# Seven products in place of eight for pairs of projection units in a two-layer decoder step

## The chip, the cores and the metric
The kernel runs on one core of one Trainium2 chip. The metric is the device time of one execution in microseconds. A core has TensorE for matmuls (PE, with its weight loads listed as PEld), VectorE (DVE), ScalarE (ACT), GpSimd (POOL) and SyncE (SP), which here issues the DMAs. Each engine takes its instructions in order; engines wait for each other by semaphores.

## The reference
Two layers work on 512 prompt tokens and 8 samples together, 520 tokens of 1024 features, in float32. In each layer:
```python
proj = rmsnorm(x, g_mix) @ w_in                  # 1024 -> 5376: u, v, q, k, v of 12 heads, two gates
A = gelu(u) * (tril(W_s) @ rmsnorm(gelu(v)) + b)  # chunks of 128 tokens
B = dilated windowed attention, 3 pairs of (window, dilation), 4 heads each, q and k normed and rotated
x = x + (sigmoid(g_a) * (A @ P_a) + sigmoid(g_b) * (B @ P_b)) @ W_o
c = causal_conv3(rmsnorm(x, g_ffn) @ W_up)        # 1024 -> 5632
x = x + (silu(c_gate) * c_val) @ W_down           # 2816 -> 1024
```
Outputs are x, the new cache rows, the last up-projected rows and the normed v of the samples.

## The kernel before
Features lie on partitions and tokens along the columns, so that a product is made of units of 128 output features by 520 tokens. A float32 product is three products of a faster format: each operand is split into a high part (cast) and a low part (what the cast left out), and a unit multiplies high by high, high by low and low by high. PE's instructions have 260 columns, so a unit over 1024 inputs takes 8 x 3 x 2 = 48 matmuls. The two halves of the tokens lie in two PSUM banks of one tile `acc`.

Weights come in the order of the list `units`: `load_raw` (L181) issues one DMA of 128 output features (512 KB for 1024 inputs) and `split` (L187) makes the high part on ACT (L193) and the low part on DVE (L194), both 1024 columns wide. `feed` (L197) keeps loads three and splits two units ahead. `dense` (L263) runs the matmuls of a unit through `products` (L243, L252). The unit is then taken out of PSUM by DVE: times 1/rms per token for input and up projections (L870, L876, L894, L1051, L1097), as a factor for the projections of the branches (L1062, L1074), added to x for the output and down projections (L1084, L1131). RMSNorm's gain is folded into x before the split (`Norm.feature`, L287), while 1/rms is applied behind the product.

The order of a layer: q, k and v of pair 2 (six units), the v half of the MLP (four), pair 1 (six), the u half (four), pair 0 (six); gates a and the A projection by turns; gates b and the B projection; eight units of W_o; then 22 tiles of the FFN, each a gate unit and a value unit of the up projection, and the down projection in three groups of eight units over 8, 7 and 7 tiles of input, the first two behind the first tile of the next group, the last at the end. Attention of the prompt and of the samples, the spatial gate and the conv history are generators in lanes; `pump` (L215), called before each k of a unit, puts their stages between the matmuls when a clock that counts PE's time says that they are due. A scheduler then orders each engine's list by a simulated timeline; evacuations and splits have priority.

On each FFN tile `up_conv` (L1093) copies ten columns on POOL (L1098), scales on ACT (L1100), adds two taps on DVE (L1102) and eight columns on POOL (L1105); `h_tile` (L1109) applies SiLU (L1120), multiplies (L1121) and splits (L1123 on ACT, L1124 on POOL).

Of the kernel before, what the change touches and what calls it, by code (L numbers as in the profile page):

```python
# [84 lines left out]
def step_kernel(ctx: ExitStack, tc: tile.TileContext, a, o):  # L85
# [59 lines left out]
    units = []  # L145
    groups = ((0, 8), (8, 15), (15, 22))
    for l in range(DEPTH):
        w_in = a["w_in"][l]
# [9 lines left out]
        for j in range(8):
            cols_of(w_in, 0, 8, O_GA + j * 128, 1)
            cols_of(a["w_a_proj"][l], 0, 4, j * 128, 1)  # L160
        cols_of(w_in, 0, 8, O_GB, NGB)
        for j in range(8):
            cols_of(a["w_b_proj"][l], 0, 2, j * 128, 1)
            if NGB + j < 8:
                cols_of(w_in, 0, 8, O_GB + (NGB + j) * 128, 1)
        cols_of(a["w_o"][l], 0, 8, 0, 8)
        for gi in range(3):
            for i in range(*groups[gi]):
                cols_of(a["w_up"][l], 0, 8, i * 128, 1)
                cols_of(a["w_up"][l], 0, 8, DFF + i * 128, 1)  # L170
# [1035 lines left out]
```

## Time and profile before
| | |
|---|---|
| time, median of 3 runs (lowest, highest) | 1585.25 us (1584.99, 1585.29) |
| profiled execution, its span | 1582.3 us, 2.95 under that median, which includes what lies around the span |
| PE busy, matmuls and transposes | 1550.8 us (98%), 12985 instructions |
| DVE, ACT, POOL busy | 934.2, 648.2, 515.6 us (59, 41, 33%) |
| PE's granted clock | 0.9 or more of full speed in all 40 slices |
| DMA | 164.24 MB, 104 GB/s in the mean |

The busy time of an engine includes the time that an instruction already started stands still. Of two neighbours on DVE or PE the end of one overlaps the start of the next, so that durations add up to more than the stretch. Two runs of this kernel agree within 0.02%.

### The profile page before, as it was taken

How to read it: one execution, taken by the hardware profiler on the slowest of the kernel's cores; microseconds unless marked ns; L12 is line 12 of the kernel's file. 1: busy time of each engine (PE TensorE's matmuls, PEld its weight loads, DVE VectorE, ACT ScalarE, POOL GpSimd, SP SyncE). 2: the span in 40 equal slices, each digit the busy share in tenths (PEclk: the TensorE clock that was granted, in tenths of full speed). 3: DMA queues.
4: the chain of work that ended last, by engine and by line, in shares of the span. 5: the costliest groups of instructions: out<-in, count | busy, mean ns of one | idle time of the engine just before them, and what ended most of it. 6: DMA issues, size and time to landing. Idle time of an engine off the chain costs nothing. (4 is left out here: it accounts for less than half of the span.)

```text
span 1582.3 us, 31439 instructions
## 1 busy us (share of the span) xinstructions
PE 1550.8 (98%) x12985; PEld 1522.5 (96%) x12985; DVE 934.2 (59%) x1344; ACT 648.2 (41%) x1155; POOL 515.6 (33%) x677
## 2 busy tenths in 40 slices
PE   8999999899999999999999999998999999999998
PEld 7989899899999999999999999998999999999998
DVE  6576856855466456556437585757655663564652
ACT  5454536334444234334435544552334441442342
POOL 3645453623222012213228272636222220220130
PEclk9999999999999999999999999999999999999999
DMA  7443333424233333332344332433332333323322
GB/s 211 132 115 112 95 107 102 152 78 131 84 94 94 94 94 86 88 95 85 108 113 126 111 125 79 120 113 113 99 115 82 93 94 94 94 84 104 92 73 70
DMA packets 294845, 164.24 MB, mean 104 GB/s; under 512 B 14143, under 2 KB 288335, under 8 KB 294687
## 3 DMA queue, kind: packets, MB, share of 16 engines
q1 hardware_dynamic: 294703, 162.24, 35.0%
q8 instruction: 102, 1.67, 0.4%
q14 instruction: 40, 0.33, 0.1%
HBM read 154.66 MB, written 10.36 MB: 104 GB/s over the span
## 5 line engine op out<-in xcount | busy, mean ns | idle before, releaser
L252 PE MATMUL acc<-t,whi 128*128 128x260 f32 x7776 | 1276.4, 285 | 11.1 <-DVE t L1051 8.7
L252 PEld LDWEIGHTS acc<-t,whi 128*128 128x128 f32 x7776 | 1070.7, 189 | 18.4 <-issue 11.6
L252 PE MATMUL acc<-t,wlo 128*128 128x260 f32 x3888 | 785.5, 284 | 0.0
L252 PEld LDWEIGHTS acc<-t,wlo 128*128 128x128 f32 x3888 | 600.4, 189 | 1.4 <-issue 0.7
L193 ACT CAST whi<-raw 128x1024 fp32r<-128x1024 f32 (+3 forms) x268 | 260.5, 973 | 457.4 <-PE acc L252 287.5
L194 DVE TENSOR_TENSOR wlo<-raw,whi 128x1024 fp32r<-128x1024 f32 (+3 forms) x268 | 323.0, 1206 | 40.3 <-ACT whi L193 22.9
L1097 DVE TENSOR_TENSOR t<-acc,t 128x520 f32<-128x520 f32 x88 | 61.5, 699 | 158.2 <-PE acc L252 158.2
L1098 POOL COPY ut<-t 128x10 f32<-128x10 f32 x88 | 30.9, 351 | 364.5 <-DVE t L1097 361.1
L1102 DVE SCALAR_TENSOR_TENSOR t<-t,cwc,t 128x511 f32<-128x511 f32 (+1 forms) x176 | 131.6, 749 | 4.9 <-ACT t L1100 1.8
L1131 DVE TENSOR_TENSOR x<-acc,x 128x520 f32<-128x520 f32 x48 | 33.5, 700 | 148.2 <-PE acc L252 148.2
L1124 POOL TENSOR_TENSOR t<-t,t 128x520 fp32r<-128x520 f32 x44 | 58.9, 1339 | 127.1 <-ACT t L1123 127.1
L300 POOL TENSOR_TENSOR t<-t,t 128x520 f32<-128x520 f32 x25 | 44.0, 1762 | 110.1 <-ACT t L299 107.5
L1100 ACT ACTIVATE t<-t,vcol,cwc 128x520 f32<-128x520 f32 x88 | 72.5, 824 | 5.8 <-DVE t L1097 5.5
L1123 ACT CAST t<-t 128x520 fp32r<-128x520 f32 x44 | 27.6, 627 | 115.2 <-DVE t L1121 115.2
L506 POOL TENSOR_TENSOR t<-t,t 128x128 f32<-128x128 f32 x96 | 56.7, 619 | 18.8 <-DVE ss L499 18.2
L1105 POOL TENSOR_TENSOR t<-t,hc 128x8 f32<-128x8 f32 x88 | 45.4, 515 | 49.7 <-ACT t L1100 49.7
L1120 ACT ACTIVATE t<-t 128x520 f32<-128x520 f32 x44 | 28.1, 639 | 81.1 <-DVE t L1102 81.1
L1075 POOL TENSOR_TENSOR t<-t,t 128x520 f32<-128x520 f32 x16 | 23.6, 1482 | 80.5 <-DVE t L1074 80.5
L653 ACT ACTIVATE t<-t,stat 128x128 f32<-128x128 f32 (+1 forms) x96 | 40.1, 420 | 22.9 <-DVE stat L650 22.7
L136 POOL TENSOR_TENSOR rr<-ss,mhalf 128x8 f32<-128x8 f32 (+1 forms) x30 | 49.0, 1632 | 0.0
L1051 DVE TENSOR_TENSOR t<-acc,t 128x520 f32<-128x520 f32 x32 | 22.2, 695 | 43.7 <-PE acc L252 43.7
L775 POOL TENSOR_TENSOR t<-t,t 128x512 f32<-128x512 f32 x24 | 35.1, 1473 | 30.3 <-DMA t<-in_cache_kv_w_dram 25.4
(195 smaller groups left out, 1172.2 us busy)
## 6 DMA issues: line engine op xcount, KB each, us to landing
raw<-in_w_up_dram SPq DMA_DIRECT2D x88, 512.0 KB
raw<-in_w_in_dram SPq DMA_DIRECT2D x84, 512.0 KB
raw<-in_w_down_dram SPq DMA_DIRECT2D x32, 448.0 KB
t<-in_cache_kv_w_dram SPq DMA_DIRECT2D x48, 256.0 KB
raw<-in_w_o_dram SPq DMA_DIRECT2D x16, 512.0 KB
raw<-in_w_down_dram SPq DMA_DIRECT2D x16, 512.0 KB
raw<-in_w_a_proj_dram SPq DMA_DIRECT2D x16, 256.0 KB
out_dram<-t SPq DMA_DIRECT2D x15, 256.0 KB
```

The source lines that it names most:

```text
L136: pool.tensor_tensor(out, in_, mhalf[: in_.shape[0], :n], op=ALU.pow)
L193: act.copy(hi[:, :nk], r)
L194: eng.tensor_tensor(lo[:, :nk], r, hi[:, :nk].bitcast(F32), op=ALU.subtract)
L252: mm = pe.matmul(acc[:, h, :H2], w[:, k], m[:, h * H2 : h * H2 + H2], start=(k == 0 and i == 0), stop=(k == last and i == 2),)
L300: eng.tensor_tensor(self.ssum[i], self.ssum[i], sq, op=ALU.add)
L506: pool.tensor_tensor(s4[:, i, :, s : s + 32], q4[:, i, :, d : d + 32], ts_[:n, i : i + 1, s : s + 32].to_broadcast([n, 4, 32]), op=ALU.mult,)
L653: act.activation(S[:, hp], S[:, hp], AF.Exp, bias=nmx[:, i : i + 1], accum_out=stat[:, 4 + i : 5 + i])
L1097: dve.tensor_tensor(v2(up), acc, rb, op=ALU.mult)
L1100: act.activation(cv, up, AF.Identity, scale=cwc[:, 2, i : i + 1], bias=vcol[:, 32 + i : 33 + i])
L1102: dve.scalar_tensor_tensor(cv[:, s:TP], up[:, : TP - s], cwc[:, j, i : i + 1], cv[:, s:TP], op0=ALU.mult, op1=ALU.add)
L1105: pool.tensor_tensor(cv[:, TP:], cv[:, TP:], hc[:, :, m], op=ALU.add)
L1124: pool.tensor_tensor(lo, cg, hi.bitcast(F32), op=ALU.subtract)
```

## The change
Where two units of 128 output features share their input, they can be computed together. The 1024 inputs are halved (1 and 2: k 0 to 3 and 4 to 7), the 520 tokens are halved (260 each), and the weights of the two units form a 2 x 2 matrix of blocks of 512 x 128. `dense2` computes seven products of such blocks, each of 4 x 3 matmuls of 260 columns into one PSUM bank: 84 matmuls for two units. The weights' side takes four sums of blocks (S1 to S4, on POOL), the input's side takes the sums of halves of x made once for each norm (`Norm.operands`), and the outputs are put together by additions out of PSUM on DVE, the first by a copy on ACT. Because sums of tokens' halves would mix two tokens' 1/rms, x is multiplied by it before the split on this path.

Pairs are: q, k and v of attention pairs 1 and 0, the MLP halves, both gates, and FFN tiles 4 to 21 (value and gate unit together): 36 a layer. The other units stay as they were, in blocks of at most four k: q, k, v of pair 2, the projections of the branches, W_o, FFN tiles 0 to 3, W_down. The down projection is cut into groups over 7, 5, 5 and 5 tiles, and the units of the first three groups are laid between later tiles: two behind each of the tiles 8 to 11, two behind 13 to 16, and 1, 1, 2 and 4 behind 18 to 21. PSUM is now five single banks `acc` and three `tp` (which take the scores too). The rings of weights hold six blocks of 4 x 128 columns, high and low, and nine raw blocks.

```diff
 def acc_tile():
-    return ps.tile([128, 2, 512], F32, tag="acc", name=nm("acc"))
+    return ps.tile([128, 512], F32, tag="acc", bufs=5, name=nm("acc"))[:, :H2]
...
+    for g, grp in enumerate(groups):
+        if grp[0] == "s":
+            _, w, c0, c1 = grp
+            loads.extend(((w, 0, 4, c0), (w, 0, 4, c1), (w, 4, 4, c1), (w, 4, 4, c0)))
+            blocks.extend((g, n) for n in ("11", "S2", "12", "S3", "22", "S1", "S4"))
+            continue
...
-    def split(u, eng=dve):
+    def split(eng=dve):
+        g, name = blocks[st["split"]]
+        def summed(p, q, op):
+            s = wp.tile([128, 4, 128], F32, tag="sum", bufs=4, name=nm("sum"))
+            with urgent():
+                pool.tensor_tensor(s, p, q, op=op)
+            return s
+        if groups[g][0] == "u":
+            r = next_raw()
+        else:
+            if name == "11":
+                d = parts4[g] = {n: next_raw() for n in ("11", "21", "22", "12")}
+                d["S1"] = summed(d["21"], d["22"], ALU.add)
+                d["S2"] = summed(d["S1"], d["11"], ALU.subtract)
+                d["S3"] = summed(d["11"], d["21"], ALU.subtract)
+                d["S4"] = summed(d["12"], d["S2"], ALU.subtract)
+            r = parts4[g][name]
...
         with urgent():
             act.copy(hi[:, :nk], r)
             eng.tensor_tensor(lo[:, :nk], r, hi[:, :nk].bitcast(F32), op=ALU.subtract)
...
+    def feed():
+        while st["split"] < len(blocks) and (st["split"] < RING or st["split"] - RING in st["used"]):
+            split()
+        while st["raw"] < len(loads) and st["raw"] < st["taken"] + RAWS - 4:
+            load_raw()
...
+    def dense2(X, g0, g1, done0, done1):
+        finish("n", "x")
+        def product(name, i, out):
+            hi, lo = block(g, name)
+            acc = acc_tile()
+            for k in range(4):
+                triple((hi[:, k], lo[:, k]), X[i][k], [acc], k == 0, k == 3)
+            used(g, name)
+            with urgent():
+                out(acc)
+        def plus(out, p):
+            return lambda acc: dve.tensor_tensor(out, acc, p, op=ALU.add)
+        a11, a12, a21, a22 = g0[:, :H2], g0[:, H2:], g1[:, :H2], g1[:, H2:]
+        def both(acc):
+            dve.tensor_tensor(a22, acc, a22, op=ALU.add)
+            dve.tensor_tensor(a12, acc, a12, op=ALU.add)
+        product("11", 1, lambda acc: act.copy(a11, acc))
+        product("S2", 6, plus(a12, a11))
+        product("12", 2, plus(a11, a11))
+        product("S3", 7, plus(a22, a12))
+        product("22", 4, plus(a21, a22))
+        product("S1", 5, both)
+        done1(g1)
+        product("S4", 3, plus(a12, a12))
+        done0(g0)
...
+        def operands(self):
+            for s in range(7):
+                    if s < 4:
+                        for xn, m in ((x1, s), (x2, s + 4)):
+                            dve.scalar_tensor_tensor(xn, x[:, m], vcol[...], self.rbc, op0=ALU.mult, op1=ALU.mult)
+                        pool.tensor_tensor(d[:, b1], x1[:, b2], x1[:, b1], op=ALU.subtract)
+                        pool.tensor_tensor(d[:, b2], x2[:, b2], x1[:, b2], op=ALU.subtract)
+                        high((s, 1), x1[:, b1])
+                        high((s, 2), x2)
+                    if 0 <= s - 1 < 4:
+                        low((k, 1), x1[:, b1], 1)
+                        low((k, 2), x2, 2, 3)
+                        dve.tensor_tensor(x1[:, b1], x2[:, b2], d[:, b1], op=ALU.subtract)
+                        dve.tensor_tensor(x1[:, b2], x2[:, b1], x1[:, b1], op=ALU.subtract)
+                        high((k, 5), d)
...
-            acc = dense(xs)
-            with urgent():
-                dve.tensor_tensor(v2(g), acc, rb, op=ALU.mult)
-            act.activation(g, g, AF.Tanh, scale=0.5)
+            dense2(X, *g, half, half)
...
+            elif i < NSTD:
+                for j in range(2):
+                    dense(xs, lambda _, *accs, j=j: unit(j, *accs))
+            else:
+                dense2(X, tmp(), tmp(), lambda up: have(1, up), lambda up: have(0, up))
...
+        for op, i, *m in ffn:
+            if op == "up":
+                h_tile(i)
+            else:
+                into_x(m[0], down(i))
```

How the lists of the engines change, at three places. DVE in the up projection, before: `wlo` is the low part of a unit's weights, `acc` the PSUM tile, `t` a work tile; L1097 takes a unit out, L1102 adds the conv's taps, L1121 multiplies.
```order
L1121 TENSOR_TENSOR t_5414<-t_5414,t_5415 128x520
L1097 TENSOR_TENSOR t_5603<-acc_5554,t_5259 128x520
L194 TENSOR_TENSOR wlo_5613<-raw_5548,whi_5612 128x1024
L1102 SCALAR_TENSOR_TENSOR t_5546<-t_5603,cwc,t_5546 128x511
L1102 SCALAR_TENSOR_TENSOR t_5546<-t_5603,cwc,t_5546 128x510
L1097 TENSOR_TENSOR t_5665<-acc_5616,t_5259 128x520
L194 TENSOR_TENSOR wlo_5683<-raw_5610,whi_5682 128x1024
L1102 SCALAR_TENSOR_TENSOR t_5547<-t_5665,cwc,t_5547 128x511
L1102 SCALAR_TENSOR_TENSOR t_5547<-t_5665,cwc,t_5547 128x510
L1121 TENSOR_TENSOR t_5546<-t_5546,t_5547 128x520
L1097 TENSOR_TENSOR t_5735<-acc_5686,t_5259 128x520
```
After, at tile 6 of layer 0: L272 is the low part of a block, from a raw block or a sum; L403, L408 and L409 are the additions out of PSUM, L1331 the taps, L1348 the product.
```order
L1331 SCALAR_TENSOR_TENSOR t_7128<-t_6977,cwc,t_7128 128x510
L272 TENSOR_TENSOR wlo_7213<-sum_7180,whi_7212 128x512
L1348 TENSOR_TENSOR t_7104<-t_7104,t_7128 128x520
L272 TENSOR_TENSOR wlo_7231<-raw_7031,whi_7230 128x512
L272 TENSOR_TENSOR wlo_7249<-sum_7182,whi_7248 128x512
L403 TENSOR_TENSOR t_7140<-acc_7164,t_7140 128x260
L403 TENSOR_TENSOR t_7140<-acc_7198,t_7140 128x260
L403 TENSOR_TENSOR t_7141<-acc_7216,t_7140 128x260
L403 TENSOR_TENSOR t_7141<-acc_7234,t_7141 128x260
L272 TENSOR_TENSOR wlo_7274<-raw_7029,whi_7273 128x512
L408 TENSOR_TENSOR t_7141<-acc_7252,t_7141 128x260
L409 TENSOR_TENSOR t_7140<-acc_7252,t_7140 128x260
```
Low parts come twice as often and half as wide, and two or three of them stand between the additions of one pair.

POOL in the up projection, before: L1098 and L1105 are the ten and the eight columns, L1124 the low part of a tile.
```order
L1124 TENSOR_TENSOR t_5939<-t_5810,t_5938 128x520
L1098 COPY ut_5260<-t_5999 128x10
L1105 TENSOR_TENSOR t_5942<-t_5942,hc_451 128x8
L1098 COPY ut_5260<-t_6061 128x10
L1105 TENSOR_TENSOR t_5943<-t_5943,hc_451 128x8
L1124 TENSOR_TENSOR t_6071<-t_5942,t_6070 128x520
L1098 COPY ut_5260<-t_6131 128x10
L1105 TENSOR_TENSOR t_6074<-t_6074,hc_451 128x8
```
After, at the same place: L254 are the sums of blocks, L1327, L1334 and L1351 what L1098, L1105 and L1124 were.
```order
L254 TENSOR_TENSOR sum_7017<-sum_7015,raw_6633 128x512
L1327 COPY ut_6098<-t_6815 128x10
L1334 TENSOR_TENSOR t_6941<-t_6941,hc_262 128x8
L254 TENSOR_TENSOR sum_7019<-raw_6633,raw_6864 128x512
L1327 COPY ut_6098<-t_6814 128x10
L1334 TENSOR_TENSOR t_6965<-t_6965,hc_262 128x8
L254 TENSOR_TENSOR sum_7021<-raw_6868,sum_7017 128x512
L254 TENSOR_TENSOR sum_7178<-raw_7027,raw_7029 128x512
L1351 TENSOR_TENSOR t_6974<-t_6941,t_6973 128x520
L254 TENSOR_TENSOR sum_7180<-sum_7178,raw_6870 128x512
L1327 COPY ut_6098<-t_6978 128x10
L1334 TENSOR_TENSOR t_7104<-t_7104,hc_262 128x8
```
Four sums stand among the five instructions that a tile had.

POOL in layer 0's input projections, where the MLP halves and the samples' attention run: before, L506 and L136 belong to the norm of q and k, L897 and L898 to GELU, L775 to the products with cached rows.
```order
L897 TENSOR_SCALAR t_977<-t_977 128x520
L506 TENSOR_TENSOR t_997<-t_996,t_659 128x4x32 x4
L898 TENSOR_TENSOR t_977<-t_977,t_855 128x520
L136 TENSOR_TENSOR rr_1034<-ss_1033,mhalf 128x8
L775 TENSOR_TENSOR t_1076<-t_1076,t_1006 128x512
L897 TENSOR_SCALAR t_1091<-t_1091 128x520
L898 TENSOR_TENSOR t_1091<-t_1091,t_983 128x520
L775 TENSOR_TENSOR t_1148<-t_1148,t_1006 128x512
L775 TENSOR_TENSOR t_1180<-t_1180,t_1006 128x512
L775 TENSOR_TENSOR t_1203<-t_1203,t_1006 128x512
```
After, L1104 and L1105 are GELU's, L957 the products with cached rows, and L254 the sums of the next pairs.
```order
L254 TENSOR_TENSOR sum_1470<-raw_1182,sum_1466 128x512
L1104 TENSOR_SCALAR t_1363<-t_1363 128x520
L957 TENSOR_TENSOR t_1383<-t_1383,t_1281 128x512
L1104 TENSOR_SCALAR t_1389<-t_1389 128x520
L1105 TENSOR_TENSOR t_1363<-t_1363,t_1114 128x520
L254 TENSOR_TENSOR sum_1751<-raw_1476,raw_1478 128x512
L1105 TENSOR_TENSOR t_1389<-t_1389,t_1113 128x520
L957 TENSOR_TENSOR t_1458<-t_1458,t_1281 128x512
L254 TENSOR_TENSOR sum_1753<-sum_1751,raw_1184 128x512
L254 TENSOR_TENSOR sum_1755<-raw_1184,raw_1476 128x512
L957 TENSOR_TENSOR t_1501<-t_1501,t_1281 128x512
L254 TENSOR_TENSOR sum_1757<-raw_1480,sum_1753 128x512
```
The sums stand between products with cached rows and GELU's instructions.

## Rows read from the trace of the kernel before
**Rows 1.** The page: span; busy us and share of each engine; the casts of the weights
```profile
span 1582.3 us, 31439 instructions
...
PE 1550.8 (98%) x12985; PEld 1522.5 (96%) x12985; DVE 934.2 (59%) x1344; ACT 648.2 (41%) x1155; POOL 515.6 (33%) x677
...
L193 ACT CAST whi<-raw 128x1024 fp32r<-128x1024 f32 (+3 forms) x268 | 260.5, 973 | 457.4 <-PE acc L252 287.5
...
```

**Rows 2.** Stretches of layer 0: length, busy us (instructions) by engine, PE clock, DMA
```profile
...
53.00:210.00 157.00, 151.93 (x1301) 144.09 (x1300) 105.39 (x177) 78.25 (x195) 81.14 (x90) 1.00 0.36 107
210.00:309.00 99.00, 94.61 (x803) 90.66 (x803) 74.28 (x145) 46.76 (x119) 62.36 (x105) 0.99 0.40 121
309.00:369.00 60.00, 58.32 (x486) 57.93 (x486) 35.42 (x49) 20.61 (x34) 13.60 (x13) 1.00 0.34 98
...
470.00:801.00 331.00, 330.92 (x2767) 330.66 (x2766) 179.77 (x216) 120.25 (x151) 67.51 (x95) 1.00 0.32 94
...
```

**Rows 3.** The same view of two stretches of 6 us
```profile
...
300.00:306.00 6.00, 1.97 (x17) 1.79 (x16) 5.82 (x8) 1.19 (x3) 6.00 (x7) 1.00 0.67 207
306.00:312.00 6.00, 6.00 (x39) 6.00 (x39) 6.00 (x8) 0.59 (x1) 2.49 (x2) 0.72 0.08 22
...
```

**Rows 4.** Timeline at 327 us: start, duration, engine, line, operands, idle time before it
```profile
...
327.05 1.31 POOL L1075 TENSOR_TENSOR t<-t,t 128x520 f32<-128x520 f32 x1 [18.56 <-DVE t L1074]
...
327.11 2.34 DVE L194 TENSOR_TENSOR wlo<-raw,whi 128x1024 fp32r<-128x1024 f32 x1 [0.20 <-ACT whi L193]
...
```

**Rows 5.** Timeline at 381 us
```profile
...
380.26 1.23 DVE L194 TENSOR_TENSOR wlo<-raw,whi 128x1024 fp32r<-128x1024 f32 x1 [0.19 <-ACT whi L193]
...
381.40 0.75 DVE L292 SCALAR_TENSOR_TENSOR t<-x,vcol,t 128x520 fp32r<-128x520 f32 x1
381.46 1.86 POOL L300 TENSOR_TENSOR t<-t,t 128x520 f32<-128x520 f32 x1 [10.01 <-ACT t L299]
...
```

**Rows 6.** Timeline at 455 us
```profile
...
455.33 1.33 POOL L1124 TENSOR_TENSOR t<-t,t 128x520 fp32r<-128x520 f32 x1 [2.93 <-ACT t L1123]
...
456.01 0.70 DVE L1097 TENSOR_TENSOR t<-acc,t 128x520 f32<-128x520 f32 x1 [1.42 <-PE acc L252]
...
```

**Rows 7.** POOL on work tiles: least, middle and greatest ns of a line
```profile
...
L506 POOL TENSOR_TENSOR t<-t,t x96: 447/476/1517, 67.3 to 1014.3; 128x128 f32<-128x128 f32 x96
...
L1124 POOL TENSOR_TENSOR t<-t,t x44: 1297/1316/1845, 434.5 to 1536.9; 128x520 fp32r<-128x520 f32 x44
...
L775 POOL TENSOR_TENSOR t<-t,t x24: 1260/1290/2297, 88.8 to 1030.0; 128x512 f32<-128x512 f32 x24
...
```

**Rows 8.** Groups by line and shape, whole span: count, busy us, mean ns, idle before
```profile
...
L194 DVE TENSOR_TENSOR wlo<-raw,whi 128x1024 fp32r<-128x1024 f32 x204 | 269.7, 1322 | 38.6 <-ACT whi L193 22.5 <-issue 1.3 <-PE acc L252 0.8
...
L1097 DVE TENSOR_TENSOR t<-acc,t 128x520 f32<-128x520 f32 x88 | 61.5, 699 | 158.2 <-PE acc L252 158.2
...
L644 DVE TENSOR_TENSOR t<-sc,cst 128x256 f32<-128x256 f32 x36 | 13.5, 411 | 0.0
...
L194 DVE TENSOR_TENSOR wlo<-raw,whi 128x512 fp32r<-128x512 f32 x16 | 11.4, 715 | 0.5 <-ACT whi L193 0.5
...
```

**Rows 9.** The same view of 53 to 210 us, DVE and then POOL
```profile
...
L515 DVE TENSOR_TENSOR t<-t,t 128x256 f32<-128x256 f32 x16 | 9.2, 601 | 1.6 <-POOL t L506 1.6
...
L518 DVE TENSOR_TENSOR t<-t,t 128x512 f32<-128x512 f32 x8 | 6.9, 867 | 0.0
L900 DVE SCALAR_TENSOR_TENSOR t<-t,t 128x520 f32<-128x520 f32 x8 | 6.7, 838 | 7.7 <-ACT t L899 7.7
...
L335 DVE TENSOR_TENSOR t<-t,t 128x520 fp32r<-128x520 f32 x4 | 2.8, 694 | 2.0 <-ACT t L334 2.0
...
L506 POOL TENSOR_TENSOR t<-t,t 128x128 f32<-128x128 f32 x32 | 20.0, 655 | 5.2 <-DVE ss L499 4.9
...
L775 POOL TENSOR_TENSOR t<-t,t 128x512 f32<-128x512 f32 x8 | 12.3, 1537 | 13.4 <-DMA t<-in_cache_kv_w_dram 8.6 <-PE tp L977 4.8
...
L556 POOL TENSOR_TENSOR t<-t,t 32x128 f32<-32x128 f32 x2 | 0.9, 450 | 0.2
...
```

More of the change, by code (lines that the diff above doesn't have):

```diff
@@ L142, in step_kernel @@
     cwc = cp.tile([128, 3, 88], F32, name="cwc")
-    units = []
-    groups = ((0, 8), (8, 15), (15, 22))
+    groups = []
+    pieces = ((0, 7), (7, 12), (12, 17), (17, 22))
+    ffn = []
+    for i in range(22):
+        ffn.append(("up", i))
+        for g, i0, ns in ((0, 8, (2, 2, 2, 2)), (1, 13, (2, 2, 2, 2)), (2, 18, (1, 1, 2, 4))):
+            if 0 <= i - i0 < 4:
+                ffn.extend(("down", g, sum(ns[: i - i0]) + j) for j in range(ns[i - i0]))
+    mix = ("g0", "g1", "b0", "g2", "b1", "b2", "g3", "b3", "b4", "b5", "b6", "b7")
@@ L147, in step_kernel, with one, two @@
     for l in range(DEPTH):
         w_in = a["w_in"][l]
-        def cols_of(w, k0, k1, c0, n):
-            units.extend((w, k0, k1 - k0, c0 + i * 128) for i in range(n))
+        def one(w, k0, nk, *cs):
+            groups.append(("u", w, k0, nk, cs))
+        def two(w, c0, c1):
+            groups.append(("s", w, c0, c1))
         for p in (2, 1, 0):
-            for off in (O_Q, O_K, O_VV):
-                cols_of(w_in, 0, 8, off + p * 256, 2)
-            if p:
-                cols_of(w_in, 0, 8, O_V if p == 2 else O_U, 4)
@@ L158, in step_kernel @@
[L158 to L170, printed above, removed]
-                if gi > 0 and i == groups[gi][0]:
-                    cols_of(a["w_down"][l], *groups[gi - 1], 0, 8)
@@ L173, in step_kernel @@
-        cols_of(a["w_down"][l], *groups[2], 0, 8)
-    raws, splits = {}, {}
-    st = {"raw": 0, "split": 0, "u": 0, "now": 0.0, "last": -9.0, "pin": False}
-    RAW_AHEAD, SPLIT_AHEAD = 3, 2
+            c = [off + p * 256 + h * 128 for off in (O_Q, O_K, O_VV) for h in range(2)]
+            if p == 2:
+                n = 3 if l == 0 else 2
+                one(w_in, 0, 8, *c[:n])
+                for i in range(n, 6):
+                    one(w_in, 0, 8, c[i])
+            else:
+                for i in range(0, 6, 2):
+                    two(w_in, c[i], c[i + 1])
@@ new lines, in qkv_units, with unit, normed @@
+            first = [0]
+            def unit(j, *accs):
+                g = tmp()
+                normed(g, accs)
+                have(first[0] + j, g)
+            dense(xs, unit, l == 0)
+            if l == 0:
+                t = tps()
+                pe.transpose(t[:, :104], vrow[:104], ident[:104, :104])
+                act.copy(vcol[:, 16:], t[:, :104])
+            for i in range(n, 6):
+                first[0] = i
+                dense(xs, unit)
+        def normed(dst, accs):
```

474 lines of the change are left out of this document (291 added, 183 removed).

## The prediction
> **What bounds the kernel now.** I read the busy times first: PE 98% of the span, DVE 59%, ACT 41%, POOL 33% [rows 1]. Then the stretches of layer 0 between landmarks: B (two MLP halves and the q, k, v of pairs 1 and 0, with most of the attention beside them) from 53 to 210 us, C (gates a) to 309, D (gates b) to 369, and the up and down projections [rows 2]. There PE is the limit nearly everywhere: 330.92 us for 2767 instructions from 470 to 801, or 119.6 ns each. So what is taken off PE is gained, as long as the other engines follow. The second thing to see is where they don't: from 300 to 306 us DVE is busy for 5.82 and POOL for all of 6 us, PE does 17 instructions, and in the 6 us behind that PE's granted clock is 0.72 [rows 3]. POOL's and DVE's work is thus not free where both are full at once.
>
> Why they can be full at half their own load is in three stretches of the timeline. POOL began a sum of 520 columns at 327.05, DVE a subtraction of 1024 at 327.11, and this took 2.34 us [rows 4] where the same instruction takes 1.23 [rows 5]: it lost 1.11, the rest of POOL's 1.31. At 381.46 it is the other way round: POOL needs 1.86 beside a DVE instruction of 0.75 that began 0.06 before, so it lost some 0.55 [rows 5]. In both cases one had the other wait until about 0.13 us before its own end. DVE instructions that read PSUM and one tile of SBUF don't take part: L1097 takes its 0.70 inside a POOL sum of 1.33 [rows 6]. So there is one resource for POOL's reads and DVE's instructions with two SBUF operands; I call it the shared port. An instruction holds it for its undisturbed time less 0.13: DVE 1.10 for 1024 columns, 0.55 for 512, 0.28 for 256, 0.62 for the three-operand form of 520; POOL 1.16 for 512 and 1.18 for 520 (1.290 and 1.316 in the middle), 0.32 for 128 (0.447 at least) [rows 7].
>
> **The change, part by part.**
>
> *PE.* 36 pairs of units a layer go from 96 matmuls to 84: 72 x 12 = 864 fewer, at 119.6 ns 103.3 us, or 1.435 us a pair (11.48 to 10.05). The transposes and all other matmuls stay. The Trainium skill (TensorE: Matmul & The Clock Gate, "Back-to-back issue gap") has columns/2.4 + 2.5 ns for the gap of single warm matmuls, 110.8 for 260 columns. By that 864 would be worth 95.7 us; the row is slower, and decides.
>
> *DVE, per pair.* Seven low parts of 512 columns in place of two of 1024: 7 x 0.715 - 2 x 1.322 = +2.4 [rows 8]. Eight additions of 260 columns out of PSUM in place of two of 520 at 0.70; 260 are not in the trace, so between half of 0.70 (+1.4) and 0.45 (+2.2); I take 0.41, the row of 256 [rows 8]: +1.9. 72 x 4.3 = 310 us.
>
> *Operands.* For each of four norms 4 steps with two three-operand products, two sums of 260 and four low parts: about 4.8 us of DVE each by the same rows, 77 us in all. DVE comes to 934 + 310 + 77 = 1320 us before overlap of neighbours, 85% of what I predict. The first pairs wait for these operands behind only three and four plain units in the input projections, behind eight in the up projections. Bounds 0 and 10 us a layer, I take 3.5, since in layer 0 DVE has 26 us of work (19 of operands, 7 for three plain units) for 17 us of PE there, but a pair starts with the operand that is ready first.
>
> *POOL.* Four sums of 512 a pair at 1.29: 5.2 us, 72 x 5.2 = 371 us, and 32 subtractions of 260 for the operands at half of 1.316, 21: from 516 to some 908. *ACT.* Half-sized casts and a copy out of PSUM; even if the 260.5 us of casts doubled [rows 1], ACT would be at 59%. It is covered by PE.
>
> *Shared port.* A pair holds it 7 x 0.55 + 4 x 1.16 = 8.5 us of its 10.05; two plain units hold it 2.2 of 11.48. This term decides. Stage by stage:
>
> B holds ten pairs, 85 us. Beside them stand DVE's eight groups of the side work, L515 to L335, 60 instructions, 26 us by the holds above, and POOL's eleven, L506 to L556, 75 instructions, 42 us [rows 9]. (POOL's powers, L136, are left out: they read at most eight columns. If they held it, 17 us more.) Sum 153 us. PE had 151.9 busy us and will have 137.5. So B is bound by the port at 153 if it never idles; full use is not to be had with two queues in order, and I take B at its old 157: its 14.4 us are lost.
>
> C and D hold eight pairs. POOL was busy 62 of 99 us in C, more than in B (81 of 157), and far less in D [rows 2]. I give these pairs half of their 11.5 us; the ends are nothing and all.
>
> Up projections: a tile with a pair holds 8.5 and four more three-operand products (2.5), a product of 520 (0.57), and POOL's low part with its small ones (1.4): 13.0 of 10.05 us of PE. The tiles 4 to 7 have no down units between them: 4 x 2.95 = 12 over, of which what was prepared ahead (six blocks, at most 8.6 us, with DVE full already) pays a little: 10 us lost. Tiles 8 to 21 have 24 down units between them, which cost PE 98 and the port 19: 14 x 13.0 + 19 = 201 of 239 us. These follow PE; that is the cover which hides the sums.
>
> Weights come in halves of 256 KB: the same bytes, at a DMA share of about a third [rows 2], hidden. Down units are cut 7, 5, 5, 5 for 8, 7, 7: as many matmuls, 32 additions in halves (0.82) for 24 (0.70) a layer, beside PE. PSUM: five banks of one product each (1.44 us) against an evacuation of 0.41; a wait of DVE of up to 4 us is covered.
>
> Sum: -103.3 + 28.7 (B, both layers) + 11.5 (C, D) + 20 (tiles 4 to 7) + 7 (operands) = -36.1. The profiled span is 1582.3, 2.95 under the median of 1585.25 that includes what lies around it; the change touches neither start nor end by more than 3 us. Prediction **1549 us**; by itself this case lies between 1520 and 1580.
>
> **The rivals.**
>
> *PE alone.* The waits at the port fall into slack: five banks, six blocks ahead. Then only the operands cost: -103 + 7, 1489 us. For it: 98% PE now, and single port waits of 1.1 us beside which PE went on [rows 4]. Against it: 153 us asked in 137.5.
>
> *The port at 85%.* Slower. DVE takes its instructions in order, so an evacuation stands behind a low part that waits for a POOL sum, which waits for the port; while both wait, the port idles. At 85% B takes 153/0.85 = 180 (+23 on 157), C and D about their old 159 (+2), tiles 4 to 7 take 52/0.85 = 61 for 46 (+15), the rest keeps its -20, operands +3.5: +23 a layer, 1631 us. It turns slower than before below about 90%. For it: [rows 3], where both were full and PE nearly stood. After a halt of 4 us the clock of 0.72 costs some 1.7 us on top. Against it: while POOL holds the port, DVE has 3.3 us of evacuations a pair that don't need it. The Trainium skill (SBUF — State Buffer, "Who interferes with whom") says that of such a DVE instruction and a GpSimd one that reads SBUF the later is blocked fully. [Rows 4, 5] agree: 2.34 for 1.23. Were it only a slowdown like the mean of 1.322 against 1.23, the case before would hold.
>
> *Sums behind a late transfer.* POOL's queue now has the sums of the next pair between the products with cached rows (L775 before). If these wait for their DMA as they do now, PE waits too, up to some 13 us a layer: 1575 us. For it: they were the port's neighbours already. Against: six blocks of lead.
>
> **How the numbers follow.** Forecast 0.43, PE alone 0.19, late transfer 0.09, port at 85% 0.29. The range of 8 in 10 goes from 1490 (half of the PE case is left out below) to 1633 (a third of the slow case above). A change under 0.2% (3.2 us) can't be told from none. Faster: 0.42 + 0.19 + 0.05 = 0.66; within 0.2%: 0.05; slower: 0.29.
>
> **What would show it.** PE with 864 fewer instructions at 119 to 121 ns between them in the down units. In B PE waiting again and again for ACT's or DVE's halves of the weights, DVE over 85% busy, its low parts of 512 at 0.9 or more in the mean in place of 0.68 to 0.72, and POOL's sums at 1.5 or more; B about 157 us long. Tiles 4 to 7 at some 12.5 us, tiles with two down units at PE's time. It is wrong if B shrinks by its 14 us (PE alone), if DVE's low parts keep 0.7 us while POOL is half busy, or if the tiles with down units halt too (port at 85%).

## The result: 11.7% slower

| | before | changed |
|---|---|---|
| time, median (lowest, highest), 4 runs each | 1585.2 us (1584.99, 1585.29) | 1770.61 us (1765.81, 1772.38) |
| ratio, 95% interval | | 1.1166 (1.115 to 1.1182) |

The forecast was 1549 us, between 1490 and 1633. The time lies above the range, on the side of the rival "port at 85%", and beyond its 1631. The page of the changed kernel, against [rows 1]: span, busy time by engine, then DVE's busy tenths and PE's granted clock in 40 slices.

```profile
span 1768.7 us, 33620 instructions
...
PE 1554.2 (88%) x12121; PEld 1504.1 (85%) x12121; DVE 1522.6 (86%) x2472; ACT 865.2 (49%) x1775; POOL 997.2 (56%) x997
...
DVE  6999979899589988999787998897984998889993
...
PEclk9889789989989899999989897888999899999999
```

PE has the 864 instructions fewer that were counted, and is not less busy (1554.2 for 1550.8 us): it worked at a lower granted clock (0.929 of full speed in the mean) and stood still for 214.5 us, where it stood for 31.5 before. DVE, forecast at 1320 us, is busy for 1522.6. The stretches of layer 0 show where, as [rows 2] do for the kernel before: A (q, k, v of pair 2), B, C, D, then F (the first four up tiles, plain), G (tiles 4 to 7) and H (tiles 8 to 21 with down units). The border of a stretch is the last evacuation of its last unit (an evacuation takes a finished product out of its PSUM bank). Columns: length, busy us (instructions) of PE, weight loads, DVE, ACT, POOL, then PE's clock and DMA.

```profile
0.00:76.20 76.20, 55.87 (x360) 52.35 (x361) 57.09 (x89) 37.50 (x67) 35.95 (x32) 0.87 0.52 138
76.20:271.20 195.00, 160.17 (x1177) 146.77 (x1176) 178.76 (x278) 98.88 (x252) 140.73 (x130) 0.86 0.32 92
271.20:388.10 116.90, 96.52 (x753) 90.08 (x752) 103.31 (x199) 55.52 (x144) 87.82 (x121) 0.93 0.34 103
388.10:442.80 54.70, 54.66 (x458) 54.45 (x457) 51.77 (x91) 29.57 (x57) 31.25 (x23) 1.00 0.39 112
485.50:553.20 67.70, 52.81 (x405) 51.95 (x404) 56.77 (x87) 30.67 (x52) 30.92 (x33) 0.90 0.20 58
553.20:610.80 57.60, 46.80 (x337) 45.84 (x336) 54.08 (x75) 28.19 (x49) 35.68 (x36) 0.88 0.24 70
610.80:848.60 237.80, 229.24 (x1874) 228.64 (x1873) 219.31 (x347) 119.57 (x209) 123.52 (x120) 0.98 0.32 92
```

B took 195 us where I had said 157. DVE was busy for 92% of it. PE's busy 160.17 us at a clock of 0.86 would be 137.7 at the full one (an estimate from that row), which is what was forecast (137.5); so some 22 us are lost to the clock, and 34.8 us PE stood still. Only D (54.7 for 60.0) is shorter by what its pairs save.

The groups by shape show DVE's low parts and POOL's sums, to be read beside [rows 7, 8]: count, busy us, mean ns.

```profile
L272 DVE TENSOR_TENSOR wlo<-raw,whi 128x512 fp32r<-128x512 f32 x336 | 332.7, 992 | 69.3 <-ACT whi L271 57.2 <-PE acc L333 6.8 <-DMA raw<-in_w_up_dram 2.3
L272 DVE TENSOR_TENSOR wlo<-sum,whi 128x512 fp32r<-128x512 f32 x288 | 263.5, 920 | 20.5 <-ACT whi L271 19.9
L403 DVE TENSOR_TENSOR t<-acc,t 128x260 f32<-128x260 f32 x360 | 149.2, 420 | 13.8 <-PE acc L333 6.2 <-ACT t L411 4.5
...
L254 POOL TENSOR_TENSOR sum<-raw,raw 128x512 f32<-128x512 f32 x144 | 222.3, 1544 | 172.8 <-DVE wlo L272 124.1 <-DMA raw<-in_w_up_dram 19.5 <-issue 15.2
```

A low part of 512 takes 0.92 to 0.99 us in the mean in place of 0.72, a sum 1.54 in place of 1.29. In the trace of the changed kernel the 206 low parts of 512 that met no POOL instruction took 0.68 us in the mean, and the 128 that began while POOL ran a sum 1.46. The additions out of PSUM, which read only one tile of SBUF, take their 0.42 (estimate 0.41).

How such waits reach PE is seen in B at 205 us. The timeline (start, duration, engine and line; in brackets the idle time before it), with PE's next product as its last line:

```profile
205.38 0.68 DVE L272 TENSOR_TENSOR wlo<-sum,whi 128x512 fp32r<-128x512 f32 x1
...
206.13 1.65 POOL L254 TENSOR_TENSOR sum<-raw,raw 128x512 f32<-128x512 f32 x1 [0.96 <-DVE wlo L272]
206.59 1.75 DVE L272 TENSOR_TENSOR wlo<-sum,whi 128x512 fp32r<-128x512 f32 x1
...
208.25 0.69 DVE L1107 SCALAR_TENSOR_TENSOR t<-t,t 128x520 f32<-128x520 f32 x1
208.47 1.60 POOL L254 TENSOR_TENSOR sum<-raw,sum 128x512 f32<-128x512 f32 x1 [0.68 <-POOL sum L254]
208.98 1.64 DVE L1214 SCALAR_TENSOR_TENSOR t<-t,t 128x520 f32<-128x520 f32 x1
...
211.31 0.70 DVE L538 TENSOR_TENSOR t<-t,t 128x520 fp32r<-128x520 f32 x1 [0.69 <-ACT t L537]
...
211.93 0.89 DVE L403 TENSOR_TENSOR t<-acc,t 128x260 f32<-128x260 f32 x2
...
212.41 0.80 PE L333 MATMUL acc<-t,whi 128*128 128x260 f32 x2 [6.36 <-DVE t L403]
```

Two evacuations of 0.42 stand at 211.93 in DVE's queue, behind a low part and a product that each lost 0.9 to 1.1 us to a POOL sum, and PE halts for 6.36 us until they free a bank. In F the same happens with the operands (layer 0, 513 us):

```profile
512.87 1.56 POOL L254 TENSOR_TENSOR sum<-raw,sum 128x512 f32<-128x512 f32 x1 [0.72 <-DMA raw<-in_w_up_dram]
...
513.23 2.71 DVE L495 TENSOR_TENSOR t<-t,t 128x520 fp32r<-128x520 f32 x3
...
515.86 1.42 DVE L506 SCALAR_TENSOR_TENSOR t<-x,vcol,t 128x520 f32<-128x520 f32 x2
...
519.82 2.25 DVE L495 TENSOR_TENSOR t<-t,t 128x260 fp32r<-128x260 f32 x4
...
521.99 0.75 DVE L1098 TENSOR_TENSOR t<-acc,t 128x260 f32<-128x260 f32 x2
522.46 0.80 PE L333 MATMUL acc<-t,whi 128*128 128x260 f32 x2 [8.95 <-DVE t L1098]
```

Nine microseconds of operands (L495, L506) and other work run on DVE ahead of two evacuations that take 0.75 us together. Around these two halts PE's granted clock was 0.60 (204.5 to 212.5 us) and 0.75 (511.0 to 522.5).

Evacuations by DVE are only one of the ways. What PE waited for, over the whole kernel and then in B of layer 0 (us in total, times, longest):

```profile
PE acc L333 <- ACT t L411: 41.6, 16, 4.1
PE acc L333 <- DVE t L1098: 40.9, 11, 8.9
PE tp L794 <- DVE t L703: 32.8, 14, 3.6
PE acc L333 <- DVE t L403: 21.7, 9, 6.4
```
```profile
PE tp L794 <- DVE t L703: 9.8, 4, 3.1
PE acc L333 <- DVE t L403: 8.9, 2, 6.4
PE tp L812 <- ACT t L873: 5.5, 1, 5.5
```

In B most halts are before attention's transposes and products (`tp`): 12 of the 34.8 us for the normed q and k, which DVE makes (L703, L704), and 13 for a `tp` bank that DVE (L826, L1205) or ACT (L873, L852) has yet to empty. Evacuations of `acc` account for 9. In G all 10.8 us of halts are for ACT's copy L411, the first evacuation of a pair. All four times it stands in ACT's queue behind a cast (L1350) that waits for a product of DVE (L1348), here at 575 us:

```profile
574.09 0.69 DVE L1348 TENSOR_TENSOR t<-t,t 128x520 f32<-128x520 f32 x1
...
574.81 0.63 ACT L1350 CAST t<-t 128x520 fp32r<-128x520 f32 x1 [1.93 <-DVE t L1348]
575.34 0.37 ACT L411 COPY t<-acc 128x260 f32<-128x260 f32 x1
...
575.76 0.80 PE L333 MATMUL acc<-t,whi 128*128 128x260 f32 x2 [4.12 <-ACT t L411]
```

So a late DVE reaches PE in three ways: by what it empties, by what it makes for attention, and through ACT's queue.

### The profile page after: what moved, and what is told of

It is laid out like the page before. It is cut to its first block, busy times and chain, and to the rows that moved or that the text cites. A ratio compares the mean times of both kernels' runs of the same rounds, so it can differ in the third digit from the quotient of the medians.

```text
span 1768.7 us, 33620 instructions
## 1 busy us (share of the span) xinstructions
PE 1554.2 (88%) x12121; PEld 1504.1 (85%) x12121; DVE 1522.6 (86%) x2472; ACT 865.2 (49%) x1775; POOL 997.2 (56%) x997
## 5 line engine op out<-in xcount | busy, mean ns | idle before, releaser
L333 PE MATMUL acc<-t,whi 128*128 128x260 f32 x7216 | 1339.4, 293 | 111.0 <-ACT t L411 41.6
L333 PEld LDWEIGHTS acc<-t,whi 128*128 128x128 f32 x7216 | 1123.3, 197 | 127.6 <-ACT t L411 45.5
L333 PE MATMUL acc<-t,wlo 128*128 128x260 f32 x3608 | 950.9, 290 | 0.0
L333 PEld LDWEIGHTS acc<-t,wlo 128*128 128x128 f32 x3608 | 666.9, 196 | 0.5 <-issue 0.2
L272 DVE TENSOR_TENSOR wlo<-raw,whi 128x512 fp32r<-128x512 f32 (+2 forms) x464 | 418.3, 904 | 89.2 <-ACT whi L271 77.0
L271 ACT CAST whi<-raw 128x512 fp32r<-128x512 f32 (+2 forms) x464 | 265.5, 576 | 320.7 <-PE acc L333 249.3
L254 POOL TENSOR_TENSOR sum<-raw,raw 128x512 f32<-128x512 f32 x144 | 222.3, 1544 | 172.8 <-DVE wlo L272 124.1
L272 DVE TENSOR_TENSOR wlo<-sum,whi 128x512 fp32r<-128x512 f32 x288 | 263.5, 920 | 20.5 <-ACT whi L271 19.9
L271 ACT CAST whi<-sum 128x512 fp32r<-128x512 f32 x288 | 177.4, 620 | 129.2 <-PE acc L333 116.9
L1331 DVE SCALAR_TENSOR_TENSOR t<-t,cwc,t 128x511 f32<-128x511 f32 (+1 forms) x176 | 171.7, 994 | 2.3 <-ACT t L1329 1.8
L403 DVE TENSOR_TENSOR t<-acc,t 128x260 f32<-128x260 f32 x360 | 149.2, 420 | 13.8 <-PE acc L333 6.2
L254 POOL TENSOR_TENSOR sum<-sum,raw 128x512 f32<-128x512 f32 x72 | 105.5, 1465 | 60.5 <-issue 43.2
L254 POOL TENSOR_TENSOR sum<-raw,sum 128x512 f32<-128x512 f32 x72 | 110.2, 1530 | 21.7 <-issue 7.7
L1351 POOL TENSOR_TENSOR t<-t,t 128x520 fp32r<-128x520 f32 x44 | 69.1, 1570 | 68.2 <-ACT t L1350 53.4
L1327 POOL COPY ut<-t 128x10 f32<-128x10 f32 x88 | 41.6, 472 | 106.1 <-DVE t L408 74.4
L835 ACT ACTIVATE t<-t,stat 128x128 f32<-128x128 f32 (+1 forms) x96 | 40.2, 423 | 31.1 <-DVE stat L832 31.1
L1350 ACT CAST t<-t 128x520 fp32r<-128x520 f32 x44 | 27.6, 627 | 55.6 <-DVE t L1348 55.5
L537 ACT CAST t<-t 128x520 fp32r<-128x520 f32 (+1 forms) x40 | 19.8, 496 | 68.3 <-DVE t L1214 26.9
```

Of the source, the lines that this page charges most:

```text
L254: pool.tensor_tensor(s, p, q, op=op)
L271: act.copy(hi[:, :nk], r)
L272: eng.tensor_tensor(lo[:, :nk], r, hi[:, :nk].bitcast(F32), op=ALU.subtract)
L333: mm = pe.matmul(b, wi, xi[:, h * H2 : h * H2 + H2], start=start and i == 0, stop=stop and i == 2,)
L403: return lambda acc: dve.tensor_tensor(out, acc, p, op=ALU.add)
L835: act.activation(S[:, hp], S[:, hp], AF.Exp, bias=nmx[:, i : i + 1], accum_out=stat[:, 4 + i : 5 + i])
```

## Experiments

The theory after the result: POOL's sums (which hold DVE off the port) and the lumps of operands (many DVE instructions in one go) fill DVE's queue; evacuations stand in it; PE halts, and the clock falls. Rivals: the rest of the rewrite costs (half blocks, five banks of one product); the mere amount of DVE's work; the wait for a sum as an operand.

All runs at a glance. Stretches are added over both layers, from the profiled execution of each (W_o, 85 us in all of them, is left out); the border of F and G shifts a little where DVE is late.

| kernel | A | B | C+D | F | G | H and last downs | time, us |
|---|---|---|---|---|---|---|---|
| changed | 128.6 | 386.1 | 345.8 | 135.9 | 114.1 | 567.7 | 1770.6 |
| 1 all plain | 95.5 | 315.3 | 322.1 | 95.8 | 92.0 | 580.4 | 1593.4 |
| 2 pairs in input only | 131.3 | 385.7 | 340.8 | 96.0 | 92.3 | 582.4 | 1721.0 |
| 3 pairs in up only | 98.4 | 315.3 | 322.6 | 136.4 | 112.8 | 568.5 | 1646.8 |
| 4 no sums | 123.3 | 337.6 | 323.0 | 129.6 | 88.9 | 543.2 | 1637.9 |
| 5 operands not urgent | 131.6 | 381.8 | 341.4 | 135.9 | 110.4 | 569.2 | 1762.6 |
| 6 no operands | 101.8 | 388.0 | 342.4 | 96.0 | 112.4 | 569.4 | 1702.3 |
| 7 sums on DVE | 127.0 | 366.2 | 332.4 | 135.2 | 110.8 | 556.0 | 1720.6 |
| 8 neither sums nor operands | 97.4 | 333.7 | 312.0 | 96.0 | 88.8 | 543.5 | 1563.9 |
| 9 sums nobody uses | 136.3 | 379.4 | 347.8 | 137.5 | 118.0 | 575.9 | 1787.4 |
| 10 as 8, three of seven blocks split | 98.9 | 309.0 | 301.4 | 95.8 | 80.8 | 541.5 | 1519.4 |
| 11 pairs in tiles 8 to 21, operands in a lump | 97.5 | 315.1 | 322.8 | 128.1 | 92.3 | 553.3 | 1602.1 |
| 12 the same, operands spread, 8 | 98.0 | 313.4 | 323.3 | 112.9 | 84.7 | 558.4 | 1583.4 |
| 13 the same, spread, 11 | 97.3 | 314.2 | 322.5 | 108.8 | 79.6 | 560.6 | 1574.7 |
| 14 as 13, sums on POOL | 97.0 | 314.9 | 324.4 | 108.8 | 85.8 | 568.4 | 1585.9 |

Runs 1 to 12 are one run each beside one of the kernel before (1584.2 to 1585.3), 13 and 14 medians of 5 and 11 runs; the stretches of 14 are from its slowest run (1591.8). The four runs of the changed kernel spread over 6.6 us, so a few microseconds between single runs show nothing. Runs 4, 6, 8, 9 and 10 leave sums or operands out, or don't use them: their times are prices of parts, not of a usable kernel.

**1, 2, 3: which part.** A pair is computed as two plain units in all stages, or in the up tiles, or in the input projections (`PAIRS_IN` lists the input projections that keep pairs, and `NSTD` is the number of plain up tiles; where a stage has no pair its operands aren't prepared):

```diff
-        def two(w, c0, c1):
-            groups.append(("s", w, c0, c1))
+        def two(w, c0, c1, kind="f"):
+            if kind in PAIRS_IN + "f":
+                groups.append(("s", w, c0, c1))
+            else:
+                one(w, 0, 8, c0)
+                one(w, 0, 8, c1)
```

> The new kernel's structure (blocks of half a unit, five PSUM banks of one product, down units between the up tiles) with every pair computed as two plain units and no operands prepared. Theory (the pairs' sums and operands crowd the port that DVE and POOL share, DVE takes its queue in order, PE starves): none of that is left, so near the kernel before, 1575 to 1600 us. Rival (the rest of the rewrite costs by itself: twice as many casts and waits, fewer banks): 1650 us or more.

> Pairs in the input projections only, all 22 up tiles plain. Theory: layer 0 of the changed kernel lost 23 us ahead of the pairs, 38 in B and 15 in C and won 8.5 in D, so 67 us a layer stay: about 1585 + 135 = 1720 us. Rival (the up tiles with their longer chain are what costs): under 1650 us.

> Pairs in the up tiles 4 to 21 only, the input projections plain. Theory: 26 us lost in the first four tiles, 12.6 in tiles 4 to 7, some 20 won in tiles 8 to 21: about 1585 + 37 = 1622 us, and with the pairs of the input projections the two excesses add up to the changed kernel's 185 us. Rival (the up tiles are what costs): 1700 us or more.

Measured: 1593.4, 1721.0 and 1646.8 us. The rest of the rewrite costs 9 us. The pairs of the input cost 127.6, those of the up tiles 53.4; both on top of 1593.4 would be 1774.4, and 1770.6 was measured: two separate losses. Run 3 was forecast at some 37 us over the kernel before and came out 62.6 over it, in the main because H gains 6 us a layer, not 20. The plain kernel's windows show what PE needs where DVE has room (F with G, H less its last 6 us, layer 0):

```profile
421.20:514.80 93.60, 93.60 (x782) 93.36 (x781) 61.38 (x105) 43.93 (x67) 23.76 (x39) 1.00 0.31 89
514.80:753.50 238.70, 238.70 (x1995) 238.70 (x1994) 142.60 (x258) 91.15 (x149) 41.13 (x68) 1.00 0.31 88
```

**4 and 9: sums left out, and sums nobody uses.**

```diff
-                d["S1"] = summed(d["21"], d["22"], ALU.add)
-                ...
+                d.update(S1=d["22"], S2=d["11"], S3=d["21"], S4=d["12"])
```

Run 9 has this line too, and still issues the four `summed(...)`.

> The changed kernel with POOL's four sums of weight quarters a pair left out (the four quarters themselves stand in their place; the output differs). All seven blocks are still cast by ACT and split by DVE, PE's work is the same. Theory (port): what a pair holds falls from 8.5 to 3.9 us, low parts of 512 back to 0.68 to 0.75 us, B near 150 and C near 85 us, tiles 4 to 7 near PE's time, the operands' loss stays: 1570 to 1630 us. Rival (the amount of DVE's work, by itself, or its wait for ACT's copies): 1720 us or more.

> The changed kernel with POOL's four sums a pair computed as before, but used by nobody: as in the run without sums, the raw quarters stand in their place (the output differs). POOL's work and its reads stay, the wait of casts and low parts for a sum is gone. Theory (the sums cost because their reads and DVE's low parts exclude each other): nearly all of the cost stays, 1730 to 1775 us, low parts of 512 at 0.9 or more. Rival (what cost was the wait for the sum as an operand): near the 1638 us of the run without sums, low parts at 0.72.

Without the sums 1637.9 us, 132.7 less (B 48, C and D 23, G 25, H 25 us of it, both layers); with sums that nobody uses 1787.4, even above the range that was expected. So it isn't the wait for a sum, it is POOL's running beside DVE. The low parts by shape, without sums and then with unused ones:

```profile
L274 DVE TENSOR_TENSOR wlo<-raw,whi 128x512 fp32r<-128x512 f32 x624 | 475.7, 764 | 124.1 <-ACT whi L273 107.4 <-PE acc L335 5.0 <-PE tp L1209 2.5
```
```profile
L278 DVE TENSOR_TENSOR wlo<-raw,whi 128x512 fp32r<-128x512 f32 x624 | 565.0, 910 | 101.8 <-ACT whi L277 93.5 <-PE acc L339 2.4 <-ACT t L475 1.9
```

764 and 910 ns for the same instruction. Another rival is that the sums make POOL's other work late. It is small beside 133 us: for what POOL makes PE waited 13.0 us in the changed kernel and 9.9 without sums, DVE 20.1 and 12.1, ACT 70.2 and 55.1 (all such waits in each trace added). In run 9 they are larger (15.5, 28.4 and 132.0), and its 17 us over the changed kernel may be that; this was not tested.

The expectation for run 4 was too low all the same, 1630 us at most: B takes 169 us a layer, not 150. Its window in layer 0:

```profile
71.30:241.00 169.70, 155.32 (x1179) 144.72 (x1179) 144.36 (x278) 100.11 (x252) 82.97 (x90) 0.89 0.35 103
```

The same 278 instructions of DVE are busy for 144.36 us here, and for 178.76 with the sums: 34 us more of waiting at the port.

**5 and 6: the operands.** In 5 their block is no longer urgent; in 6 they are left out:

```diff
-                with urgent():
+                if True:
```
```diff
+            for n, c, o in ((1, b1, 0), (2, b1, 4), (3, b2, 4), (5, b1, 0), ...):
+                self.X[n].extend((h[:, c], lo[:, c]) for h, lo in self.xs[o : o + 4])
+            return
```

> The changed kernel, with the operands' instructions (products, sums, high and low parts of the halves of the features) taken out of the urgent class, so that the evacuations of PSUM go ahead of them in DVE's queue. Theory (operands ahead of evacuations stop PE in A and F, some 20 us at each of four places): part of it comes back, 1700 to 1740 us. Rival (the first pair waits for its operands wherever they stand, so that the order is nothing): 1760 to 1790 us.

> The changed kernel without the preparation of operands: the high and low parts of the features, which are there anyway, stand in their place (the output differs). PE, casts, sums and evacuations are the same. Theory: A and F go back to what they take with all plain units (59.6, 29.8 and 47.9, 41.8 us), so 16.6 + 23 + 19.8 + 26.8 = 86 us less, near 1685 us, and B, C and G stay as they are. Rival (A and F are long because the first pairs' sums and blocks are prepared there): over 1740 us.

Without operands 1702.3, 68.3 less, nearly all of it in A (26.8) and F (39.9); F is at the plain 96.0 again. (The expectation was 1685: A kept 6 us, B and C and D didn't gain.) Not urgent: 1762.6, 8 us less, against 1700 to 1740 expected. The edit hardly moved the operands: in its trace they still run ahead of the same evacuation, and PE halts for 9.07 us in F where it halted for 8.95. So this run doesn't show what another order would do; that the lump is at fault in F is shown by runs 11 to 13; for A, where pairs follow after three or four plain units, no run spreads the operands.

**7: sums on DVE.**

```diff
-                pool.tensor_tensor(s, p, q, op=op)
+                dve.tensor_tensor(s, p, q, op=op)
```

> The changed kernel with the four sums a pair on DVE in place of POOL. Theory (port and the wait of one engine for the other): the hold of a pair falls from 8.5 to some 6.1 us and low parts go back to 0.70 to 0.75, but DVE's queue has 7 x 0.70 + 7 x 0.42 + 4 x 0.68 = 10.6 us a pair for PE's 10.05: B near 175 us, G near 56, in all 1700 to 1770 us. Rival (DVE's amount of work alone is what costs): 2.7 us a pair more, 72 x 2.7 = 195 on top of 1771, over 1900 us.

1720.6 us, 50 less, as expected, although DVE now does all 288 sums as well. It is even less busy than before, 1484.2 us for 1522.6:

```profile
PE 1535.9 (89%) x12121; PEld 1486.2 (86%) x12121; DVE 1484.2 (86%) x2760; ACT 871.3 (51%) x1775; POOL 581.1 (34%) x709
```
```profile
L277 DVE TENSOR_TENSOR wlo<-raw,whi 128x512 fp32r<-128x512 f32 x336 | 253.9, 757 | 48.3 <-ACT whi L276 45.8 <-PE acc L338 1.2
```

**8 and 10: what is left.** 8 joins 4 and 6. In 10 the four sum blocks of a pair (not three, as the expectation says) moreover take the high and low part of the block before, so that four casts on ACT and four low parts on DVE go:

```diff
+            if name[0] == "S":
+                splits[g, name] = st["prev"]
+                st["split"] += 1
+                return
```

> The changed kernel with neither the sums nor the operands (raw quarters and the features' own parts stand in their place; the output differs). Theory (two separate costs that add): 1638 us without the sums, less the 86 us of A and F: 1550 us or a little under, since fewer halts leave the clock up. Rival (the saving of PE is had in full once both are gone): 1593 - 103 = 1490 us.

> The changed kernel without sums and operands and, on top, with the casts and low parts of the three sum blocks left out: these products take the high and low parts of the block before (the output differs). DVE has 7 x 0.72 - 4 x 0.72 = 2.2 us a pair less, PE's instructions are the same. Theory (what is left of the loss without sums and operands is the amount of work in DVE's queue, 87% of B): B from 165 to some 145 us, C from 105 to some 92, in all 1490 to 1515 us, where PE's count puts it (1593 - 103 = 1490). Rival (seven separate products and their evacuations cost PE, by banks or copies): 1540 us or more.

8: 1563.9, 14 above what was expected; the two savings (132.7 and 68.3) add up to 201.0, and 206.7 were measured. 10: 1519.4, just above its range: the amount of work in splitting blocks is a third, smaller cost (44.5 us). DVE's busy time fell by 186 us and ACT's by 162, so this run doesn't tell which of the two it was. PE's saving is then had in G (80.8 us; 8 pairs at 10.05 are 80.4) and H, not in B (154.5 us a layer, where run 1's 157.7 less PE's 14.4 would be 143). In layer 0's B there (153.2 us, DVE busy for 114) PE is busy for 146.2 at a clock of 0.97 and halts for 7.0: some 4 us for what DVE makes for the transposes (L713, L714), and 3 for `tp` banks that ACT empties. None is for a bank of `acc`. Why these come late there is open. This run also shows what the lower clock costs: the same 12121 instructions of PE,

```profile
PE 1481.1 (98%) x12121; PEld 1444.8 (95%) x12121; DVE 1029.7 (68%) x2056; ACT 676.7 (45%) x1423; POOL 476.6 (31%) x677
```

in 1481.1 us at a mean clock of 0.987, in 1554.2 at 0.929: 73 us (the ratio of the two clocks by itself would make it 92, an estimate from these figures).

**11 to 14: the pairs where they pay.** Pairs in tiles 8 to 21 alone (`PAIRS_IN` empty), sums on DVE, operands not urgent, eight plain up tiles in place of four; the operands' seven steps come at once (11), or one by one over the plain tiles, with 8 (12) or 11 (13) on the builder's clock between them:

```diff
-NSTD = 4
+NSTD = 8
-                yield -0.7
+                yield -0.7 if self.gofs < 16 else -11.0
```

> Pairs in the up tiles 8 to 21 only, where down units stand between them; sums on DVE, the operands' instructions not urgent, all else plain units. Theory: 1593 less 6 to 11 us a layer in tiles 8 to 21; the operands' 19 us of DVE fall into eight plain tiles, where DVE is 65% busy, in one lump, and cost 5 to 15 us a layer: 1580 to 1605 us. Rival (operands always cost their 20 us): 1610 us or more.

> As the kernel with pairs in tiles 8 to 21 and sums on DVE, but with the seven steps of the operands spread over the eight plain tiles, about one a tile. Theory (operands cost only where they come in one lump ahead of evacuations): hidden in the main, 1570 to 1585 us, so about the kernel before or a little under. Rival (operands always cost their 20 us a layer): 1610 us or more.

> Pairs in the up tiles 8 to 21 only, sums on DVE, the seven steps of the operands spread over nearly all of the eight plain tiles (11 in place of 8 on the builder's clock between them). Theory (operands are free where DVE has slack all along): F and G from 98.7 to 94 to 97 us, in all 1574 to 1583 us, under the kernel before by 0.2 to 0.7%. Rival (the operands' amount costs what it costs, spread or not): 1581 to 1586 us as with a spacing of 8, no difference from before.

> The same with the sums on POOL. Theory (an exclusion by POOL holds DVE's whole queue for 1.2 us, a sum in DVE's own queue only for 0.7): tiles 8 to 21 at 238 us in place of 233, in all 8 to 14 us more than with the sums on DVE, 1584 to 1595 us. Rival (where down units stand between the pairs, either is hidden): within 3 us of the kernel with sums on DVE.

1602.1, 1583.4, then 1574.7 (1572.5 to 1576.02): 0.9934 of the kernel before, 95% interval 0.992 to 0.9947, all three as expected. **Run 13 beats both kernels**, the one before by 0.66%. F with G, then H, in layer 0:

```profile
423.00:517.00 94.00, 94.00 (x784) 93.77 (x784) 83.92 (x143) 50.76 (x82) 37.83 (x47) 1.00 0.30 85
517.00:751.40 234.40, 226.80 (x1873) 225.80 (x1872) 213.89 (x397) 119.89 (x208) 44.81 (x70) 0.99 0.32 92
```

DVE does 22.5 us more in F and G than in the plain kernel, and PE doesn't wait at all (94.00 of 94.00): spread, the operands are free. What PE still loses in H is 7.3 us in layer 0 before ACT's copy of a pair's first product, the way by ACT's queue again; another order on ACT was not tried. In 11 no pair waits for them before tile 8, and yet F loses 32 us over both layers; so it is the lump in DVE's queue that stops PE, not a pair that waits for its operands. With the sums on POOL (14) the median is 1585.9, 11 us more, as expected, and 1.0007 of before (0.9996 to 1.0017); in its H POOL is busy for 123 us in place of 45, and DVE, with 51 instructions fewer on record, for 218.19 in place of 213.89:

```profile
521.10:760.00 238.90, 228.90 (x1861) 228.12 (x1860) 218.19 (x346) 118.58 (x208) 123.33 (x120) 0.97 0.32 91
```

## Why the prediction was wrong

The sum had forecast -36 us against the kernel before; measured were +185. Its terms in both layers, each measured against the plain kernel of the same structure (run 1):

| term | forecast | measured |
|---|---|---|
| operands (A and F) | +7 | +73.2 |
| B | 0 | +70.8 |
| C and D | -11.5 | +23.7 |
| tiles 4 to 7 (-11.5 + 20) | +8.5 | +22.1 |
| tiles 8 to 21, last downs | -40.2 | -12.7 |
| the rest of the rewrite (run 1 against the kernel before) | 0 | +9.2 |

- *"864 fewer, at 119.6 ns"*: right in the count, and in D the gain is there. Nothing in this step was wrong; PE wasn't the limit.
- *Operands, "bounds 0 and 10 us a layer, I take 3.5"*: failed. It is 36.6 a layer, and run 6 shows 33 of them to be the operands'. I weighed DVE's 26 us against PE's 17 for A, but in F gave them the eight plain units as cover. DVE has 30 of 48 us of work in F with plain units [run 1: 61.38 in F and G], so 19 to 27 more in one lump leave none, and evacuations stand behind the lump.
- *B, "full use is not to be had with two queues in order, and I take B at its old 157"*: failed. This term and the operands, each by itself, are larger than the gain of 36 us in the forecast. By my holds the port was asked for 153 us of the 195, 78%. I had summed the holds of the port as if DVE's other work could run under POOL's hold. It can't: the queue is in order, so the limit is DVE's whole work (144.4 us without sums) and its added waits at the port (34) together, 178.8 us, 92% of the stretch. The argument set against the slow rival, "while POOL holds the port, DVE has 3.3 us of evacuations a pair that don't need it", is refuted by the timeline at 206 us: the evacuations stand behind the instruction that waits. I had also not seen that PE would halt before attention's transposes and products, which is the larger part in B. The Trainium skill (SBUF — State Buffer, "Who interferes with whom") says of DVE and GpSimd that "only the shared port pair causes contention, and it's an exclusive lock", and has a DVE instruction with two SBUF inputs contend with a GpSimd instruction that reads SBUF. The trace agrees: 1.75 us for a low part of 0.68 that began in a POOL sum.
- *C and D, "half of their 11.5 us"*: wrong for the same reason: C, where POOL has most work of its own, lost 38 us, D gained 14. Without the sums C loses 12.
- *"A wait of DVE of up to 4 us is covered"*: the waits were longer, with halts of 6.36 and 8.95 us, and ACT's copy, which the forecast called covered, was itself the largest single wait of PE (41.6 us).
- *Tiles 4 to 7*: 14.3 us a tile for 13.0; right in kind.
- *Tiles 8 to 21, "the cover which hides the sums"*: half wrong. PE is busy for 229 of 238 us there, yet the gain is 12.7 of 40.2; without sums it is 37.2 (run 4). PE's halts there are again for ACT's copy (8.6 us in layer 0).
- *Clock*: priced at 1.7 us for a halt of 4 us in the rival alone and left out of the sum; against run 10, where PE stands still for 36 us in all, PE's busy time is 73 us longer.
- The rival *"port at 85%"*, given 0.29, named the mechanism that decided. It came out at 1631 since it had the port's use too high (85% for 78% in B), the operands at 3.5 and tiles 8 to 21 at their full gain.
- The rival of sums behind a late transfer is not what came: PE's waits for a DMA are 5.9 us in all, at the start, and POOL's products with cached rows waited 5.1 us for theirs, less than before (25.4).
- *The rest of the rewrite* (halved blocks, other groups of down units, five banks) was put at nothing and cost 9 us.

What it had right: low parts at 0.9 or more, sums at 1.5 or more, DVE over 85%, D at PE's time. What it named as proof against itself, that tiles with down units halt too, is what came.

## What to carry to other kernels

When a scheme saves work on the bound engine by giving more to another, put the other engine's whole queue, its waits at a shared port included, against the time of each stage; B still lost to it here with DVE at 144 of 170 us (without sums). Instructions that could run while their engine's queue stands at the port don't, since the queue is in order; and a copy on a third engine can stand behind an instruction that waits for the late one. Prepared operands belong spread over the work before. Of two engines that shut each other out, the one that needed less time for a sum was the better place here (DVE 0.71 to 0.88 us in run 7, POOL 1.47 to 1.54), though it was the busier one: with both, and the saving sought only where DVE has room, 864 instructions less cost 185 us and 336 less gained 10.
